# Mean pooling over 512 MiB: loads of 63 KB per partition in pairs of one run, double stores of 31.5 KB runs, the last double store on SP's queue

## The chip, the cores and the metric

The kernel runs on one core of one Trainium2 chip. A core has several engines that run side by side; three matter here. VectorE (DVE) does the additions, ScalarE (ACT) the scaling and also issues most stores, and SyncE (SP) issues the loads. The data are moved between the chip's main memory (HBM) and the core's working memory (SBUF, 128 partitions) by 16 DMA engines. Each transfer that SP or ACT issues is cut into one packet per contiguous run and shared among the 16 DMA engines; SP's transfers stand in one queue on each of them (q1 in the profile), ACT's in another (q10).

The metric is the device time of one execution in microseconds (us); lower is better. The kernel before has a median of 1554.53 us over three runs (1554.42 to 1555.98).

## The reference

The input x has 64 x 256 rows of 8192 float32 numbers, 536.87 MB. Kernel size and stride are both 4, so each output is the mean of four neighbours, no two outputs share an input, and the output has 64 x 256 x 2048 numbers, 134.22 MB.

```python
x = np.random.randn(64, 256, 8192).astype(np.float32)   # kernel_size = stride = 4
out_len = (length - kernel_size) // stride + 1           # 2048
for i in range(out_len):
    start = i * stride
    output[:, :, i] = np.mean(x[:, :, start : start + kernel_size], axis=2)
```

Since the row length is a multiple of 4, the whole input can be treated as one flat run of numbers, and every stretch whose length is a multiple of 4 becomes a stretch of a quarter of its length in the flat output.

## The kernel before

The flat input has 134,217,728 numbers, 1,048,576 for each of the 128 partitions. It is cut into 64 blocks of 128 x 16384 numbers (`FULL`), each one contiguous piece of memory of 8 MB, in which partition p takes the p-th 64 KB. The last two blocks are laid out together: partition p has one run of 128 KB there (`xe`, line 67), whose first half is block 62 and whose second half is loaded in three pieces of 8192, 4608 and 3584 numbers (`TAIL`).

`fetch(i)` (line 72) takes one of two input buffers (`xin`, `bufs=2`) and lets SP issue the load of block i. Two loads are issued ahead. The loop at line 84 then handles one block a turn:

- `sums` (line 55): two DVE additions. The first (line 57) adds even and odd neighbours in place, 16384 numbers to 8192; the second (line 58) adds neighbours again and writes 4096 sums into half of an output buffer `ot` (8192 numbers a partition, two buffers).
- `fetch(i + 2)`: SP issues the load of block i + 2 into the buffer that has just been summed. SP's instruction waits until DVE is done with that buffer.
- `nc.scalar.mul` (line 97): ACT multiplies by 1/4 in place, and `store` (line 50) lets ACT issue the store.

The first 8 blocks (`SINGLE`) are stored one by one. From then on two blocks are scaled and stored together once the second is summed: 8192 numbers a partition, but in memory they are two separate runs of 16 KB, since the two blocks lie apart (`"(b p m) -> p b m"`, line 52).

At the end, block 62 is scaled by ACT (line 92) and not stored yet. The three pieces of the last block follow (line 101): the first is summed, scaled by ACT and stored by SP together with block 62, as one run of 24 KB (line 110); the second is scaled by ACT and stored by ACT; the last is scaled by DVE (line 105), which has just summed it, and stored by ACT (line 112).

The order on each engine is the program's order. SP's queue holds all loads and the one store at line 110; ACT's queue holds the other 37 stores. A planner fills in the waits from the use of the buffers: a load waits for the sums that read its buffer before, and a sum into `ot` waits for the store that read that buffer before.

Of the kernel before, what the change touches and what calls it, by code (L numbers as in the profile page):

```python
# [1 line left out]

# [4 lines left out]


FULL = 16384
PAIR = 2  # L10

SINGLE = 8

TAIL = (8192, 4608, 3584)


@with_exitstack
def kernel(
    ctx: ExitStack,
    tc: tile.TileContext,  # L20
    x: bass.AP,
    kernel_size: bass.AP,
    stride: bass.AP,
    out: bass.AP,
):
    nc = tc.nc
    K, S = int(kernel_size), int(stride)
    assert K == S == 4
    B, C, L = x.shape
    assert L % K == 0  # L30
    P = nc.NUM_PARTITIONS
    dt = x.dtype
    add, mult = mybir.AluOpType.add, mybir.AluOpType.mult


    xf = x.rearrange("b c l -> (b c l)")
    of = out.rearrange("b c l -> (b c l)")
    blocks = B * C * L // P // FULL
    assert blocks * P * FULL == B * C * L and sum(TAIL) == FULL and blocks % PAIR == 0
    M = FULL // K  # L40

    pin = ctx.enter_context(tc.tile_pool(name="xin", bufs=2))
    pout = ctx.enter_context(tc.tile_pool(name="res", bufs=2))

    def load(xt, a, w):

        src = xf[P * a : P * (a + w)].rearrange("(p m) -> p m", p=P)
        nc.sync.dma_start(out=xt, in_=src)  # L48

    def store(engine, o, a, n, m):  # L50

        dst = of[P * a : P * (a + n * m)].rearrange("(b p m) -> p b m", b=n, p=P)
        engine.dma_start(out=dst, in_=o.rearrange("p (b m) -> p b m", b=n))

    def sums(xt, o):
        w = xt.shape[1]
        nc.vector.tensor_tensor(out=xt[:, : w // 2], in0=xt[:, ::2], in1=xt[:, 1::2], op=add)  # L57
        nc.vector.tensor_tensor(  # L58
            out=o, in0=xt[:, : w // 2 : 2], in1=xt[:, 1 : w // 2 : 2], op=add
        )  # L60

    xs = {}

    end = blocks - 2
    xe = xf[P * end * FULL :].rearrange("(p m) -> p m", p=P)
    oe = of[P * end * M :].rearrange("(p m) -> p m", p=P)
    edges = [FULL + sum(TAIL[:i]) for i in range(len(TAIL) + 1)]
    pieces = list(zip(edges[:-1], edges[1:]))  # L70

    def fetch(i):
        xt = xs[i] = pin.tile([P, FULL], dt, name="xt")
        if i < end:
            load(xt[:, :], i * FULL, FULL)
        elif i == end:
            nc.sync.dma_start(out=xt[:, :], in_=xe[:, :FULL])
        else:
            for a, b in pieces:
                nc.sync.dma_start(out=xt[:, a - FULL : b - FULL], in_=xe[:, a:b])  # L80

    fetch(0)
    fetch(1)
    for i in range(blocks - 1):
        k = i % PAIR
        if k == 0:
            ot = pout.tile([P, PAIR * M], dt, name="ot")
        sums(xs.pop(i)[:, :], ot[:, k * M : (k + 1) * M])
        if i + 2 < blocks:
            fetch(i + 2)  # L90
        if i == end:
            nc.scalar.mul(ot[:, :M], ot[:, :M], 1.0 / K)  # L92
        elif k == PAIR - 1 or i < SINGLE:

            n = 1 if i < SINGLE else PAIR
            o = ot[:, (k + 1 - n) * M : (k + 1) * M]
            nc.scalar.mul(o, o, 1.0 / K)  # L97
            store(nc.scalar, o, (i + 1 - n) * M, n, M)

    xt = xs.pop(blocks - 1)  # L100
    for a, b in pieces:
        o = ot[:, a // K : b // K]
        sums(xt[:, a - FULL : b - FULL], o)
        if b == 2 * FULL:
            nc.vector.tensor_scalar(out=o, in0=o, scalar1=1.0 / K, scalar2=None, op0=mult)  # L105
        else:
            nc.scalar.mul(o, o, 1.0 / K)  # L107
        if a == FULL:

            nc.sync.dma_start(out=oe[:, : b // K], in_=ot[:, : b // K])  # L110
        else:
            nc.scalar.dma_start(out=oe[:, a // K : b // K], in_=o)


# [1 line left out]
_INS = ['x', 'kernel_size', 'stride']  # L116
_OUTS = [((64, 256, 2048), 'float32')]

_NUMBERS = {'kernel_size': 4, 'stride': 4}


# [26 lines left out]
```

## Time and profile before

| what | value |
|---|---|
| median of three runs | 1554.53 us (1554.42 to 1555.98) |
| profiled execution, first to last instruction (span) | 1552.9 us |
| what lies around the span, against the median | 1.6 us (1554.53 - 1552.9) |
| DVE busy | 840.8 us, 54% |
| ACT busy | 226.7 us, 15% |
| bytes read and written | 536.87 MB and 134.22 MB, 432 GB/s over the span |
| DMA packets | 18435 |
| one full block on DVE, line 57 and line 58 | 8692 ns and 4425 ns |
| scaling of a double on ACT | 7029 ns |
| full load, issue to landing | 35.1 us (median of 63) |
| double store, issue to landing | 51.8 us (median of 27) |
| single store, issue to landing | 31.7 us (median of 8) |

The profile is of one execution. It lists no time of its own for that execution beside the span; the difference to the median of the runs is what is put around the span here.

How to read it: a row of the timeline has the start of an instruction, its duration, its engine and line, and in brackets how long the engine had been idle before it and what ended that. A row of the windows has a stretch of time, the busy time of DVE, ACT and POOL in it with the number of instructions, the granted TensorE clock (TensorE is not used here), the share of the 16 DMA engines that was busy, and the GB/s they moved. The share can come out slightly above 1.00, since a packet's record can overlap the next one's. The chain is the work that ended last, followed back from the end; it goes through whatever released the next step, which need not be the resource that limits the whole. The trace also holds a record of each DMA packet, with its size, its queue, its start and its duration.

### The profile page before, as it was taken

The numbers are of one execution on the slowest core, as the hardware profiler recorded it, in microseconds if no ns is written. First come the engines' busy times: TensorE is split into PE (matmuls) and PEld (weight loads), VectorE is DVE, ScalarE is ACT, GpSimd is POOL, SyncE is SP. The second block draws the span as 40 slices with busy tenths as digits, with TensorE's granted clock in tenths as the row PEclk, the third lists the DMA queues.
The fourth block names the chain that finished last, engine by engine and source line by source line (L and its number), as shares of the span: only waits on it lengthen the run. The fifth ranks groups of instructions, "written<-read, shape, count | busy, mean of one in ns | idle before, by whom it ended". The sixth has DMA issues, their size and how long they took to land.

```text
span 1552.9 us, 476 instructions
## 1 busy us (share of the span) xinstructions
DVE 840.8 (54%) x133; ACT 226.7 (15%) x39; POOL 0.2 (0%) x4
## 2 busy tenths in 40 slices
DVE  3646556546465464654646546455464554645546
ACT  1111101110111101111011110111101111011111
POOL 0000000000000000000000000000000000000000
DMA  9999999999999999999999999999999999999999
GB/s 415 421 433 439 439 439 439 412 446 436 421 433 433 445 437 438 433 422 430 439 437 434 437 427 425 439 432 438 438 419 435 434 436 438 442 425 435 425 432 406
DMA packets 18435, 671.12 MB, mean 432 GB/s; under 512 B 1664, under 2 KB 1664, under 8 KB 1920
## 3 DMA queue, kind: packets, MB, share of 16 engines
q1 hardware_dynamic: 9648, 540.02, 80.3%
q10 hardware_dynamic: 8784, 131.07, 19.7%
q14 instruction: 3, 0.02, 0.0%
HBM read 536.87 MB, written 134.22 MB: 432 GB/s over the span
## 4 chain that ended last, share of the span: by engine, by line
DMA 73%; DVE 26%; issue 0%; SPq 0%
DMA xt<-in_x_dram 73%; DVE xt L57 18%; DVE ot L58 9%; SPq L80 0%; DVE ot L105 0%; SPq L48 0%
## 5 line engine op out<-in xcount | busy, mean ns | idle before, releaser
L57 DVE TENSOR_TENSOR xt<-xt 128x8192 f32<-128x8192 f32 (+1 forms) x66 | 556.6, 8433 | 701.4 <-DMA xt<-in_x_dram 701.4
L97 ACT ACTIVATE ot<-ot 128x8192 f32<-128x8192 f32 (+1 forms) x35 | 218.7, 6249 | 1289.1 <-DVE ot L58 1289.1
L58 DVE TENSOR_TENSOR ot<-xt 128x4096 f32<-128x4096 f32 (+1 forms) x66 | 283.5, 4296 | 3.9
L92 ACT ACTIVATE ot<-ot 128x4096 f32<-128x4096 f32 x1 | 3.6, 3617 | 16.6 <-DVE ot L58 16.6
L107 ACT ACTIVATE ot<-ot 128x2048 f32<-128x2048 f32 (+1 forms) x2 | 3.1, 1537 | 10.2 <-DVE ot L58 10.2
L97 ACT ACT_TABLE_LOAD x1 | 1.3, 1283 | 0.7 <-PEq L129 0.7
L105 DVE TENSOR_SCALAR ot<-ot 128x896 f32<-128x896 f32 x1 | 0.6, 627 | 0.0
L129 POOL MEMSET const-bfloat16-1.0<- 128x1 bf16 x1 | 0.1, 102 | 0.0
L129 POOL MEMSET const-uint8-127<- 128x1 uint8 x1 | 0.1, 102 | 0.0
L129 POOL MEMSET const-float32-0.0<- 128x1 f32 x1 | 0.1, 99 | 0.2 <-issue 0.2
L129 POOL MEMSET const-float32-1.0<- 128x1 f32 x1 | 0.1, 99 | 0.0
## 6 DMA issues: line engine op xcount, KB each, us to landing
out_dram<-ot ACTq DMA_DIRECT2D x27, 4096.0 KB, 51.8
out_dram<-ot ACTq DMA_DIRECT2D x8, 2048.0 KB, 31.7
xt<-in_x_dram SPq DMA_DIRECT2D x1, 4096.0 KB, 24.9
out_dram<-ot SPq DMA_DIRECT2D x1, 3072.0 KB, 13.6
xt<-in_x_dram SPq DMA_DIRECT2D x1, 2304.0 KB, 35.0
xt<-in_x_dram SPq DMA_DIRECT2D x1, 1792.0 KB, 38.6
xt<-in_x_dram SPq DMA_DIRECT2D x63, 35.1
out_dram<-ot ACTq DMA_DIRECT2D x1, 576.0 KB, 7.6
```

The lines of the kernel that those rows point to most:

```text
L57: nc.vector.tensor_tensor(out=xt[:, : w // 2], in0=xt[:, ::2], in1=xt[:, 1::2], op=add)
L58: nc.vector.tensor_tensor(out=o, in0=xt[:, : w // 2 : 2], in1=xt[:, 1 : w // 2 : 2], op=add)
L92: nc.scalar.mul(ot[:, :M], ot[:, :M], 1.0 / K)
L97: nc.scalar.mul(o, o, 1.0 / K)
L105: nc.vector.tensor_scalar(out=o, in0=o, scalar1=1.0 / K, scalar2=None, op0=mult)
L107: nc.scalar.mul(o, o, 1.0 / K)
L129: nc = _bacc.Bacc("TRN2", target_bir_lowering=False, num_devices=1)
```

## The change

The block becomes 128 x 16128 numbers, 63 KB a partition. The work is now a list of stretches, each of them one contiguous piece of memory in which a partition has one run:

- `FIRST`: one block by itself, stored by itself (4032 numbers a partition).
- 31 `PAIR`s of two blocks: partition p has a run of 126 KB, of which the first load takes the first 63 KB and the second load the rest. The means of both are one run of 31.5 KB a partition and go out in one store.
- `LAST`: one block and the three pieces of 8192, 4608 and 3584 numbers, as one run a partition.

That makes 1 + 62 + 1 = 64 full loads and 3 pieces (64 x 16128 + 16384 = 1,048,576 numbers a partition). The buffers keep their sizes (16384 and 8192 numbers a partition, two of each). The steps of a turn keep their order: sums, the fetch two ahead, scaling, store. The order at the end is another: the last pair's double store is issued by SP, after the loads of the last block and of the three pieces (`i == len(fills) - 3`); the last block is stored by itself, by SP; each of the three pieces is stored by itself, by ACT. The last piece is scaled by DVE as before.

```diff
-FULL = 16384
-PAIR = 2
-SINGLE = 8
-TAIL = (8192, 4608, 3584)
+FULL = 16128
+FIRST = (FULL,)
+PAIR = (FULL, FULL)
+LAST = (FULL, 8192, 4608, 3584)
+PAIRS = 31
...
+    for widths in stretches:
+        n = sum(widths)
+        xs = xf[P * at : P * (at + n)].rearrange("(p m) -> p m", p=P)
+        os = of[P * at // K : P * (at + n) // K].rearrange("(p m) -> p m", p=P)
+        edges = [sum(widths[:i]) for i in range(len(widths) + 1)]
+        pieces = list(zip(edges[:-1], edges[1:]))
+        if widths is LAST:
+            fills += [(xs, os, pieces[:1], n), (xs, os, pieces[1:], n)]
+        else:
+            fills += [(xs, os, [p], n) for p in pieces]
+        at += n
...
+        xt = tiles[i] = pin.tile([P, 16384], dt, name="xt")
+        for a, b in pieces:
+            nc.sync.dma_start(out=xt[:, a - base : b - base], in_=xs[:, a:b])
+
+    def scale_and_store(engine, ot, os, a, b, last=False):
+        o = ot[:, a // K : b // K]
+        if last:
+            nc.vector.tensor_scalar(out=o, in0=o, scalar1=1.0 / K, scalar2=None, op0=mult)
         else:
...
+            nc.scalar.mul(o, o, 1.0 / K)
+        engine.dma_start(out=os[:, a // K : b // K], in_=o)
...
+    for i, (xs, os, pieces, n) in enumerate(fills):
+        base = pieces[0][0]
+        if base == 0:
+            ot = pout.tile([P, 8192], dt, name="ot")
+        xt = tiles.pop(i)
+        end = i >= len(fills) - 2
+        for a, b in pieces:
+            sums(xt[:, a - base : b - base], ot[:, a // K : b // K])
+            if end:
+                engine = nc.sync if a == 0 else nc.scalar
+                scale_and_store(engine, ot, os, a, b, last=b == n)
+        if i + 2 < len(fills):
+            fetch(i + 2)
+        if not end and pieces[-1][1] == n:
...
+            engine = nc.sync if i == len(fills) - 3 else nc.scalar
+            scale_and_store(engine, ot, os, 0, n)
```

More of the change, by code (lines that the diff above doesn't have):

```diff
@@ L37 @@
     of = out.rearrange("b c l -> (b c l)")
-    blocks = B * C * L // P // FULL
-    assert blocks * P * FULL == B * C * L and sum(TAIL) == FULL and blocks % PAIR == 0
-    M = FULL // K
+    stretches = [FIRST] + [PAIR] * PAIRS + [LAST]
+    assert sum(map(sum, stretches)) * P == B * C * L
     pin = ctx.enter_context(tc.tile_pool(name="xin", bufs=2))
     pout = ctx.enter_context(tc.tile_pool(name="res", bufs=2))
[L45 to L53, printed above, removed]
     def sums(xt, o):
@@ L60, in sums @@
         )
[L62 to L70, printed above, removed]
-    def fetch(i):
[L73 to L101, printed above, removed]
+    fills = []
+    at = 0
+    for widths in stretches:
[9 more added lines that the diff above has]
+        at += n
+    tiles = {}
+    def fetch(i):
+        xs, _, pieces, _ = fills[i]
+        base = pieces[0][0]
[3 more added lines that the diff above has]
+    def scale_and_store(engine, ot, os, a, b, last=False):
         o = ot[:, a // K : b // K]
-        sums(xt[:, a - FULL : b - FULL], o)
-        if b == 2 * FULL:
+        if last:
             nc.vector.tensor_scalar(out=o, in0=o, scalar1=1.0 / K, scalar2=None, op0=mult)
@@ L107 @@
             nc.scalar.mul(o, o, 1.0 / K)
[L108 to L112, printed above, removed]
+        engine.dma_start(out=os[:, a // K : b // K], in_=o)
+    fetch(0)
+    fetch(1)
+    for i, (xs, os, pieces, n) in enumerate(fills):
+        base = pieces[0][0]
+        if base == 0:
[12 more added lines that the diff above has]
+            scale_and_store(engine, ot, os, 0, n)
 _INS = ['x', 'kernel_size', 'stride']
```

## The prediction

> **What bounds the kernel now.** I read the page's head first (busy shares, DMA rate), then its chain, then the windows, then the chain and the timeline at three places: the start, one steady stretch, the end.
>
> ```profile
> DVE 840.8 (54%) x133; ACT 226.7 (15%) x39; POOL 0.2 (0%) x4
> DMA packets 18435, 671.12 MB, mean 432 GB/s; under 512 B 1664, under 2 KB 1664, under 8 KB 1920
> q1 hardware_dynamic: 9648, 540.02, 80.3%
> q10 hardware_dynamic: 8784, 131.07, 19.7%
> ```
>
> No compute engine is full, and the two data queues together hold the 16 DMA engines for 100.0% of the span. q1 is SP's queue (the loads), q10 ACT's (the stores). The chain says "DMA 73%; DVE 26%", which looks as if DVE shared the bound. It does not: the chain goes through DVE because SP issues load i+2 when DVE has summed tile i, while load i+1 is still moving. The windows show this.
>
> ```profile
> 300.00:400.00 100.00, 52.47 (x8) 14.06 (x2) 0.00 (x0) 1.00 1.01 435
> 700.00:800.00 100.00, 55.69 (x10) 14.06 (x2) 0.00 (x0) 1.00 1.00 433
> 1300.00:1400.00 100.00, 55.77 (x9) 14.06 (x2) 0.00 (x0) 1.00 1.00 434
> 1500.00:1520.00 20.00, 9.58 (x2) 7.03 (x1) 0.00 (x0) 1.00 1.00 433
> 1520.00:1540.00 20.00, 14.81 (x5) 5.53 (x2) 0.00 (x0) 1.00 1.00 429
> 1545.00:1552.90 7.90, 1.11 (x2) 0.00 (x0) 0.00 (x0) 1.00 0.69 291
> ```
>
> The last two columns are the DMA share and GB/s: 1.00 and about 433 everywhere, with a hole only in the last 7.9 us. So time can come from three places alone: fewer bytes (none here: both kernels read 536.87 MB and write 134.22 MB), less cost per packet, or less idle time at the ends.
>
> What a packet costs, apart from its bytes, comes from two cadences. The landing of a load is where DVE's next line-57 add starts.
>
> ```profile
> 22.62 8.69 DVE L57 TENSOR_TENSOR xt<-xt 128x8192 f32<-128x8192 f32 x1 [22.62 <-DMA xt<-in_x_dram]
> 41.93 8.69 DVE L57 TENSOR_TENSOR xt<-xt 128x8192 f32<-128x8192 f32 x1 [6.17 <-DMA xt<-in_x_dram]
> ...
> 1542.33 2.02 DVE L57 TENSOR_TENSOR xt<-xt 128x1792 f32<-128x1792 f32 x1 [0.17 <-DMA xt<-in_x_dram]
> ...
> 1545.51 0.63 DVE L105 TENSOR_SCALAR ot<-ot 128x896 f32<-128x896 f32 x1
> ```
>
> The timeline above gives start, duration, engine, line and, in brackets, the idle time; the chain below gives start, duration and work.
>
> ```profile
> 763.73 8.70 DVE xt L57
> ...
> 860.41 8.70 DVE xt L57
> ```
>
> Before the first store, one load takes 41.93 - 22.62 = 19.31 us: per DMA engine 8 packets of 65,536 B and one for the semaphore. In the steady stretch four loads and two stores take 860.41 - 763.73 = 96.68 us, 48.34 us a pair: per engine 16 load packets, 16 store packets of 16,384 B and 3 semaphore packets, 35 packets, 1,310,720 B. Two equations with a rate r and a cost c per packet: 19.31 = 524,288/r + 9c and 48.34 = 1,310,720/r + 35c give r = 27.22 B/ns and c = 5.2 ns. The trace's records of single packets agree: 65,536 B took 2418 ns, 16,384 B 611, 3,584 B 140, which is 27.2 B/ns and 8.6 ns besides; the records overlap a little, which is why the two shares can add up to more than 1.00. From the first data packet to the last in these records is 1550.0 us; a rate of 27.2 B/ns needs 1542.0 us for an engine's 41.94 MB. Take off 0.9 us of slow first packets (3.0 to 3.4 us each) and 1.2 us in which engines had finished one after another at the end, and 5.9 us are left for 1152 packets on each engine: 5.1 ns. I use that.
>
> The Trainium skill, DMA: Bandwidth & Descriptors, in "Where 436 GB/s comes from", makes the ceiling 16 ports of 32 B at 850 MHz, 435.2 GB/s; the steady rows (433 to 435) lie just under it, so the trace agrees.
>
> **The change part by part.** The sum goes against the profiled execution: span 1552.9 us. Its own time is not listed apart from the span; the median of the three runs, 1554.53, lies 1.6 us above it, and I carry that 1.6 over.
>
> *Packets.* Loads: 64 of 63 KB a partition and 3 tail pieces, 67 x 128 = 8576 data packets (66 x 128 = 8448 before). Stores: 1 single, 31 doubles now in one run, 4 at the end, 36 x 128 = 4608 (8192 before, each double being two 16 KB runs a partition). Semaphore packets: 103 DMAs x 16 = 1648 (104 x 16 = 1664). Sum 14,832 against 18,432 outside the small third queue, 927 against 1152 an engine. 225 packets fewer at 5.1 ns: **-1.1 us**. Bounds: 0 if the fixed cost hangs on bytes or on the count of loads, -1.9 us at the 8.6 ns that a single record shows. I take 5.1 because it is the mean over the whole execution.
>
> *Compute.* DVE adds as many elements in one pair of instructions more: 65,536-byte tiles cost 8.69 + 4.42 us, so 63 KB tiles 8.56 + 4.36. ACT's scaling of a double takes 7.03 x 63/64 = 6.92 us; 8 singles become doubles. None of it is on the path while a load is queued. The cover: load i+2 is issued 13.0 us after load i lands, and load i+1 needs 19.0 us (19.31 x 63/64) even with no store beside it. That leaves 6 us, less 1.4 us from an issue to its first packet (issue at 0.73, first packet near 2.1) and about 1 us of spread between engines. If the cover were gone, each microsecond missing would cost up to 1 us in each of 60 loads; I cost it at nothing.
>
> *Store order in the steady stretch.* In the records load and store packets alternate, so a 64 KB and a 16 KB packet give stores a fifth of the rate, and a double store needs 16 x (2.418 + 0.611) = 48.5 us, near the 51.8 us to landing that the page shows. With 63 KB and 31.5 KB packets it needs 8 x (2.380 + 1.194) = 28.6 us, about 31 to landing. The output buffer is wanted again some 62 us after the first scaling, so no new wait. The engines do the same bytes either way: 0.
>
> *The seam at the end.* The second of the last pair now stores through SP, behind the load of the last 63 KB block and the three pieces; on SP's queue the next store (of that block) waits behind it for ACT, and nothing else does. ACT's queue is left with the three small stores. The last loads no longer share the engines with a store, so the last one lands earlier. Remaining then: 4.13 + 2.06 + 1.05 + 0.59 + 0.46 = 8.29 MB, 19.1 us at 434 GB/s, where the kernel before had some 9 us left. So the last landing comes about 10 us earlier, near 1532, and DVE's end is covered: block (12.9 us) and first piece (6.7) make it late, pieces two and three follow, done about 8 us after the last landing, when SP's queue still has 10 us of stores. What is late next is the engines' own store work, so the 10 us buy nothing. Left to win is the idle end: of the 7.9 us at a share of 0.69, 2.4 us are idle, most of it after the last packet and in the spread of 1.2 us. The last packets stay the 3.5 KB ones of the same last store. Bounds: -0.7 (spread gone) to +0.5 (19 us at the 422 GB/s which 291/0.69 makes of that window, 2.6% under 433). I take **0**, between them.
>
> *Start.* Same first load but for 1 KB. Only one store instead of eight comes early; the engines have loads queued meanwhile. 0.
>
> Sum: 1552.9 - 1.1 = 1551.8 span, 1554.53 - 1.1 = **1553.4 us**.
>
> The Trainium skill, DMA: Bandwidth & Descriptors, "Why small descriptors are slow", puts the fixed cost at about 3 cycles a packet, 3.5 ns at its 850 MHz; by it the packets would save 0.8 us and the sum be 1553.7. The cadence says 5 ns, and the measurement goes first.
>
> **Rivals.**
>
> 1. *No saving.* The 31.5 KB runs are cut in two on the way, or the fixed cost is not a packet's. Against it: records of 14,336, 18,432, 24,576 and 32,768 B each are one packet. Then 8 more load packets an engine and the end's bound: 1554.5 to 1555.1. Chance 0.12.
>
> 2. *Slower: the new pitch.* Loads of a pair read 63 KB of every 126 KB instead of one closed block, so the engines walk other addresses. It decides when it costs 3.1 + 1.1 = 4.2 us, 8 ns on each of an engine's 512 full load packets (0.35%). For it: the window 1520 to 1540, in which the last block and pieces with a pitch of 128 KB land, has 429 GB/s. Against it: the 128 full packets of that block took 2418 ns each, as all others. Priced at 429 against 433 over the kernel: 671.1/0.429 - 671.1/0.433 = 14.5 us, 1553.4 + 14.5 = 1568. Chance 0.09. [...]
>
> 3. *Faster: the mixing was the cost.* If what the mixed stretch loses against loads alone is paid in the alternation of queues, it could shrink further: a pair costs 48.34 - 2.5 x 19.31 = 0.07 us more than loads alone, 32 pairs make 2.1 us. With the end's spread of 1.2 and half of the loads' own 2.2 us (0.035 us above 27.2 B/ns, x 64) it is 4.4 us: 1550.1. All of this would have to come together. Chance 0.05.
>
> **How the numbers follow.** Forecast (1551.9 to 1554.5): 0.74. It is taken from 1554.53 with the largest gains, -1.9 and -0.7, at its low end and no gain at its high one. Rival 1 adds 0.12 up to 1555.1. The range 1551.8 to 1555.9 holds these with the spread of the runs shown (1554.42 to 1555.98), and leaves rivals 2 and 3 out. 0.2% is 3.1 us, about what a measurement of this kernel can tell from no change: below 1551.4 faster, above 1557.6 slower. Forecast and rival 1 both lie within: 0.86, of which I give 0.01 to faster for the forecast's tail. Same 0.85, slower 0.09 (rival 2), faster 0.06 (rival 3 and that tail).
>
> **What would show it.** Packets near 14,835, 432 to 433 GB/s, DMA share 1.00 up to the last 2 or 3 us. Landing of a double store from 51.8 to about 31 us. DVE still idle for landings alone, and the last line-57 add starting near 1532 instead of 1542, with no earlier end in proportion. Two loads, one store and their pair taking 47.56 us (1,290,240 B at 27.2 B/ns and 27 packets at 5.1 ns): four loads and two stores in 95.1 us. The prediction is wrong if a stretch has a share of 1.00 at under 430 GB/s (longer packets, rival 2), if shares under 0.97 appear between loads (the cover of 6 us was too thin), or if more than 3 us go idle at the end.

## The result: slower by 0.7%

The changed kernel took 1565.55 us in the median of four runs (1561.93 to 1568.02), the kernel before 1554.52. The ratio is 1.0068, with a 95% interval of 1.0056 to 1.0080. A second measurement of the same code (e14 below) gave 1570.12, 1.0103 (1.0086 to 1.0120). The prediction was 1553.4 and no change that can be told; the time lies above its range of 1551.8 to 1555.9.

The page of the changed kernel has the packets that were forecast, and still no compute engine is full. Busy times, packets and the two data queues:

```profile
DVE 840.7 (54%) x135; ACT 226.1 (14%) x36; POOL 0.2 (0%) x4
DMA packets 14835, 671.12 MB, mean 430 GB/s; under 512 B 1648, under 2 KB 1648, under 8 KB 1904
q1 hardware_dynamic: 9936, 543.07, 80.8%
q10 hardware_dynamic: 4896, 128.03, 19.0%
out_dram<-ot ACTq DMA_DIRECT2D x30, 4032.0 KB, 32.4
```

14,835 packets as forecast, and a double store lands 32.4 us after its issue (forecast: about 31). But the mean rate is 430 GB/s and not 432. The windows show where (the last two columns are the DMA share and GB/s):

```profile
200.00:300.00 100.00, 51.67 (x8) 13.84 (x2) 0.00 (x0) 1.00 1.00 434
400.00:500.00 100.00, 56.20 (x9) 13.84 (x2) 0.00 (x0) 1.00 1.00 434
900.00:1000.00 100.00, 55.71 (x9) 13.84 (x2) 0.00 (x0) 1.00 1.00 428
1100.00:1200.00 100.00, 55.64 (x9) 13.84 (x2) 0.00 (x0) 1.00 1.00 430
1300.00:1400.00 100.00, 51.67 (x8) 13.84 (x2) 0.00 (x0) 1.00 0.99 427
1550.00:1562.30 12.30, 0.00 (x0) 0.00 (x0) 0.00 (x0) 1.00 0.58 244
```

Up to about 600 us the DMA engines move 434 GB/s, after that 427 to 434, at a share of 0.99 to 1.01 up to 1500 us: the engines are as busy as before and get less done. At the end 12.3 us have a share of 0.58 (before: 7.9 us at 0.69). The chain gives the same by the pair; each of these lines is DVE's first add (line 47) on the second block of a pair, first early, then late in the execution:

```profile
134.08 8.57 DVE xt L47
...
181.67 8.57 DVE xt L47
...
229.32 8.57 DVE xt L47
...
276.96 8.57 DVE xt L47
...
324.56 8.57 DVE xt L47
```
```profile
1234.89 8.57 DVE xt L47
...
1282.66 8.57 DVE xt L47
...
1330.69 8.57 DVE xt L47
...
1378.47 8.57 DVE xt L47
...
1426.55 8.57 DVE xt L47
```

Early a pair takes (324.56 - 134.08)/4 = 47.62 us, against 47.56 forecast. Late it takes (1426.55 - 1234.89)/4 = 47.92 us.

The trace's records of single packets say which packets are longer. In the kernel before a full load packet took 2418 ns nearly always; only 22 of 8000 after the start were more than 2% longer. In the changed kernel the usual 63 KB packet took 2380 ns, but 404 of 8128 were more than 2% longer, up to 3728 ns. Some 70 of these lie at the first two stores; the next ten starts of a store bring only a few, and the bulk comes after about 600 us. Nearly all belong to the second load of a pair and lie where the double store of the pair before begins: each engine's load packet that is under way just before its first store packet, and often the next. In the middle of a store nearly all packets have their usual length.

With these records the difference between the two profiled executions can be added up (the changed kernel's took 1564.11 us, so the table does not hold the rest up to its median). The columns are us from the first data packet to the last, per engine; "lengthened" is the time by which packets exceed the usual length of their size; "idle" is engine time without a packet, most of it in the last 10 us:

| term | before | changed |
|---|---|---|
| bytes at 27.2 B/ns | 1542.0 | 1542.0 |
| packets per engine x 5.1 ns | 1152: 5.9 | 927: 4.7 |
| slow first packets | 0.7 | 0.7 |
| lengthened packets | 0.6 | 8.1 |
| idle | 1.1 | 3.9 |
| sum; measured | 1550.3; 1550.0 | 1559.4; 1559.3 |

The packets saved 1.2 us, as forecast. Lengthened packets took back 7.5 and the uneven end 2.8. (The prediction took 0.9 us for the slow first packets; with the table's terms a packet costs 4.8 ns in the kernel before and 4.9 in the changed one, which is why the sums come out slightly high.)

### The profile page after: what moved, and what is told of

It is laid out like the page before. It is cut to its first block, busy times and chain, and to the rows that moved or that the text cites. A ratio compares the mean times of both kernels' runs of the same rounds, so it can differ in the third digit from the quotient of the medians.

```text
span 1562.3 us, 477 instructions
## 1 busy us (share of the span) xinstructions
DVE 840.7 (54%) x135; ACT 226.1 (14%) x36; POOL 0.2 (0%) x4
## 2 busy tenths in 40 slices
DMA packets 14835, 671.12 MB, mean 430 GB/s; under 512 B 1648, under 2 KB 1648, under 8 KB 1904
## 4 chain that ended last, share of the span: by engine, by line
DMA 71%; DVE 27%; issue 0%; DVEq 0%; SPq 0%
DMA xt<-in_x_dram 71%; DVE xt L47 18%; DVE ot L48 9%; DVEq L48 0%; DVE ot L80 0%; SPq L75 0%
## 5 line engine op out<-in xcount | busy, mean ns | idle before, releaser
L47 DVE TENSOR_TENSOR xt<-xt 128x8064 f32<-128x8064 f32 (+2 forms) x67 | 556.7, 8309 | 705.1 <-DMA xt<-in_x_dram 705.1
L82 ACT ACTIVATE ot<-ot 128x8064 f32<-128x8064 f32 (+3 forms) x35 | 224.8, 6422 | 1320.6 <-DVE ot L48 1320.6
L48 DVE TENSOR_TENSOR ot<-xt 128x4032 f32<-128x4032 f32 (+2 forms) x67 | 283.6, 4234 | 4.1
## 6 DMA issues: line engine op xcount, KB each, us to landing
out_dram<-ot ACTq DMA_DIRECT2D x30, 4032.0 KB, 32.4
```

Source lines behind the costliest of these rows:

```text
L48: nc.vector.tensor_tensor(out=o, in0=xt[:, : w // 2 : 2], in1=xt[:, 1 : w // 2 : 2], op=add)
```

## The experiments

The theories, as they stood at the start. **A**: a store that starts on an empty store queue lengthens the load packets under way. The kernel before does this once or twice, because its double store takes as long as a pair (51.8 us to landing, 48.3 a pair); the changed kernel does it in each pair, because its stores take 31.5 KB for 63 KB of load and are through after 30 us. **B**: the loads' pitch of 126 KB. **C**: packets off the 64 KB grid. **D**: the new order at the end. A "restart" below is such a start on an empty store queue. The times of the full runs differ by about 1% or less, so what is compared is, beside the time, the lengthened packets of one profiled execution each; between executions of one kernel these vary (8.1 us in the changed kernel above, 10.1 in e14).

### e1: the double store as two transfers of 15.75 KB packets

```diff
-        engine.dma_start(out=os[:, a // K : b // K], in_=o)
+        h = 2 if b - a == 2 * FULL else 1
+        w = (b - a) // K // h
+        for j in range(h):
+            engine.dma_start(
+                out=os[:, a // K + j * w : a // K + (j + 1) * w],
+                in_=o[:, j * w : (j + 1) * w],
+            )
```

> The changed kernel, but a double store goes out as two transfers of 15.75 KB a partition instead of one of 31.5 KB; loads and end unchanged. Theory A (onset): each time the store queue starts again after having run empty, the load packet under way on each engine is lengthened, which costs the changed kernel some 8 us over 31 pairs. Here a double store needs 16 x (2.380 + 0.601) = 47.7 us beside loads, and a pair takes 47.6, so the queue does not run empty: mean full load packet 2383 ns or less (2397 in the changed kernel), time 1553 to 1556. Theory B (the loads' pitch of 126 KB) and theory C (packets of 63 KB off the 64 KB grid): loads unchanged, so 2395 to 2400 ns and 1562 to 1568.

Measured: 1557.98 us, 1.0019 (1.0010 to 1.0028). That is 2 us above theory A's range and 4 us below that of B and C. The mean full load packet is 2383 ns, 1.0 us of lengthened packets in all after the start, and the pairs are even. In the records the time in each pair without a store packet falls from 23 us in the changed kernel to 2.4 us or less, one load packet. The same place in the chain as above:

```profile
1228.08 8.57 DVE xt L47
...
1275.69 8.57 DVE xt L47
...
1323.30 8.57 DVE xt L47
...
1370.91 8.57 DVE xt L47
...
1418.52 8.57 DVE xt L47
```

Each pair takes 47.61 us. The loads are those of the changed kernel, with pitch and 63 KB packets, so neither B nor C explains its loss. The kernel has 279 packets more on each engine than the changed one, 1206 against 927, and is 7.6 us faster. It stays 3.4 us over the kernel before; by the same sum its profiled execution has 0.3 us from packets, 0.4 from lengthened packets and 0.9 from idle time. That execution was the fastest of ten, and what the others have besides is not seen.

### e2: 64 KB blocks at a pitch of 128 KB

```diff
-FULL = 16128
+FULL = 16384
...
-    stretches = [FIRST] + [PAIR] * PAIRS + [LAST]
+    stretches = [PAIR] * PAIRS + [LAST]
```

> The changed kernel with blocks of 64 KB and no single block in front: 31 pairs of 64 KB loads at a pitch of 128 KB, double stores in one run of 32 KB, end unchanged. Theory A: a double store needs 8 x (2.418 + 1.213) = 29 us of a 48.2 us pair, so the store queue runs empty in each pair and the loss stays: 1561 to 1568, full load packets 10 to 20 ns over 2418 in the mean. Theory B: a pitch again, 1560 to 1570. Theory C: back on the 64 KB grid, 1553 to 1556.

Measured: 1569.63 us, 1.0091 (1.0068 to 1.0115); the mean full load packet is 2449 ns instead of 2418, and 15.7 us of packets are lengthened on an engine. Both are more than theory A had said (up to 1568 us and 20 ns longer packets), and by this time alone B would do as well. The size off the grid (C) is not the cause: on the grid the loss is at least as large.

```profile
300.00:400.00 100.00, 52.48 (x8) 16.29 (x3) 0.00 (x0) 1.00 1.00 431
400.00:500.00 100.00, 52.47 (x8) 15.90 (x3) 0.00 (x0) 1.00 1.00 429
1200.00:1300.00 100.00, 52.47 (x8) 14.06 (x2) 0.00 (x0) 1.00 0.99 425
```

Here the loss is there from the first pairs on: 429 to 431 GB/s already between 300 and 500 us.

### e3: 63 KB blocks, each one closed piece of memory

```diff
+            if n == 2 * FULL:
+                xs = xf[P * at : P * (at + n)].rearrange("(b p m) -> p b m", b=2, p=P)
+                os = of[P * at // K : P * (at + n) // K].rearrange("(b p m) -> p b m", b=2, p=P)
             fills += [(xs, os, [p], n) for p in pieces]
...
```

(The lines left out take the load and the store from these pieces.)

> Blocks of 63 KB as in the changed kernel, but each block one closed piece of memory as in the kernel before, so a double store is one transfer of two runs of 15.75 KB a partition; end unchanged. Theory A: the store queue does not run empty (47.7 us against 47.6), 1553 to 1556, load packets 2383 ns or less. Theory B: no pitch, 1553 to 1556. Theory C: still 63 KB packets, 1562 to 1568.

Measured: 1556.81 us, 1.0011 (1.0002 to 1.0021), mean full load packet 2383 ns, 0.9 us of lengthened packets; a double store lands late again:

```profile
out_dram<-ot ACTq DMA_DIRECT2D x30, 4032.0 KB, 51.3
```

B is undone here, C is not, and the loss is gone; with e1 this leaves the stores.

### e4: the last double store on ACT's queue

```diff
-            engine = nc.sync if i == len(fills) - 3 else nc.scalar
-            scale_and_store(engine, ot, os, 0, n)
+            scale_and_store(nc.scalar, ot, os, 0, n)
```

> The changed kernel with the last double store on ACT's queue, beside the last loads, instead of on SP's queue behind them. The changed kernel has 3.7 us of idle engine time at its end against 1.2 before. Theory D (the seam makes the end uneven): 2 to 3 us less than the changed kernel, 1559 to 1565. Theory A without D: the end's idle time comes from engines that the onsets have driven apart, so the time stays at 1562 to 1568 and one engine still lags 4 us or more.

Measured: 1569.91 us, 1.0099 (1.0083 to 1.0114), beside 1570.12 for the changed kernel measured again. The end has 3.1 us of idle time in its last 10 us, hardly less than the changed kernel's 3.7. D falls. The time lies above both forecasts, and 15.8 us of packets are lengthened. Until its end this is the changed kernel, yet its engines drift apart, and longer packets and a lower rate appear, much earlier:

```profile
200.00:300.00 100.00, 51.67 (x8) 13.84 (x2) 0.00 (x0) 1.00 0.99 426
```

So when the loss sets in differs between executions of the same steps.

### e5, e6, e7: short loads beside short stores

If A is right as it stands, a restart costs whatever the packets' size. In e5, the kernel before loads 64 KB in two transfers of 32 KB, so its 16 KB stores take a third of the engines and run dry. e6 adds `SINGLE = 62`, so the same stores come in more starts. e7 takes e5 and cuts the stores to 8 KB packets, so the queue stays busy.

```diff
-        nc.sync.dma_start(out=xt, in_=src)
+        for h in range(0, w, w // 2):
+            nc.sync.dma_start(out=xt[:, h : h + w // 2], in_=src[:, h : h + w // 2])
...
-            nc.sync.dma_start(out=xt[:, :], in_=xe[:, :FULL])
+            for h in (0, FULL // 2):
+                nc.sync.dma_start(out=xt[:, h : h + FULL // 2], in_=xe[:, h : h + FULL // 2])
```

> The kernel before with each full load issued as two transfers, the first and the second 32 KB of each partition's 64 KB; stores as before, 16 KB a packet. 63 x 9 packets more on each engine at 5.1 ns make 2.9 us, 1557.4 without any other loss. Theory A (each restart of an empty store queue costs about 8/31 = 0.26 us): a double store now needs 16 x (1.213 + 0.611) = 29 us of 48.4, so the queue runs empty 35 times (8 singles, 27 doubles), 9 us more: 1563 to 1571. Theory A' (it is the long store packet of 31.5 KB and not the empty queue): 1556 to 1559.

> As e5, but the first 62 blocks are all stored one by one, so the same 16 KB packets go out in 62 separate starts instead of 35. Theory A: 62 restarts at 0.26 us, 16 us over 1557.6: 1568 to 1580, clearly slower than e5. Theory E (not the restart but the time during which stores take a third of the engines costs, whatever the number of starts): the same as e5 within 2 us.

> As e5, but each store goes out as two transfers with packets of 8 KB, so a double store needs 32 x (1.213 + 0.309) = 48.7 us beside the loads and the queue does not run empty. About 550 store packets more on each engine, 2.8 us. Theory A: only the packets' cost, 1557.4 + 2.8 = 1560 (1558 to 1562.5), faster than e5 with more packets. Theories A' and E: slower than e5 by those 2 to 3 us.

Measured: e5 1559.51 us (1.0033), e6 1560.50 (1.0039), e7 1560.55 (1.0039). The queue does run dry in e5; its double store lands after 31.8 us:

```profile
out_dram<-ot ACTq DMA_DIRECT2D x27, 4096.0 KB, 31.8
out_dram<-ot ACTq DMA_DIRECT2D x8, 2048.0 KB, 18.3
```

Yet all packets together are lengthened by only 2.3 us on an engine in e5 and 1.8 in e6, and 1.1 and 0.7 of it fall in the first 45 us; each later start costs 0.04 us or less. Theory A as I had put it falls, with its 9 and 16 us. (e6 is within 1 us of e5, as theory E said, but neither has a loss of the changed kernel's size.) e7 has 0.5 us of lengthened packets and 1098 packets more on each engine than the kernel before: at 5.1 ns that is 5.6 us, measured 1560.55 - 1554.45 = 6.1. The packet's price holds far outside the range it was read from. That e7 would be faster than e5, as theory A said, did not come true.

### e8: the new end on the kernel before

```diff
+            nc.sync.dma_start(out=oe[:, :M], in_=ot[:, :M])
...
-            store(nc.scalar, o, (i + 1 - n) * M, n, M)
+            store(nc.sync if i == end - 1 else nc.scalar, o, (i + 1 - n) * M, n, M)
...
-        if a == FULL:
-
-            nc.sync.dma_start(out=oe[:, : b // K], in_=ot[:, : b // K])
-        else:
-            nc.scalar.dma_start(out=oe[:, a // K : b // K], in_=o)
+        nc.scalar.dma_start(out=oe[:, a // K : b // K], in_=o)
```

> The kernel before with the changed kernel's end alone: the last double store on SP's queue behind the last loads, block 62 stored by itself by SP, the first piece by ACT. Theory D (the seam costs): 1556 to 1558, as the two variants of 63 KB without restarts (1556.8 and 1558.0) still lie 2 to 3 us over the kernel before. Without D: 1553.5 to 1555.

Measured: 1554.55 us, 1.0001 (0.9992 to 1.0010). The third part of the change neither costs nor gains, as forecast, and the 3.4 and 2.3 us that e1 and e3 keep are not from it.

### e9, e10, e11: which of three conditions is needed

All start from e2, which has long loads (64 KB), long stores (32 KB) and a restart in each pair. e9 makes the stores short by leaving out the second half of each pair's means, e10 makes the loads short, and e11 keeps both long and removes the restart: it reads half of the input and stores each result twice. e9 and e11 do other work in all, so their times are not compared, and each is a single execution.

```diff
 e9
+        if b - a == 2 * FULL:
+            b, o = a + FULL, o[:, : FULL // K]
 e10
-            nc.sync.dma_start(out=xt[:, a - base : b - base], in_=xs[:, a:b])
+            c = FULL // 2 if b - a == FULL else b - a
+            for h in range(a, b, c):
+                nc.sync.dma_start(out=xt[:, h - base : h - base + c], in_=xs[:, h : h + c])
 e11
-PAIRS = 31
+PAIRS = 15
...
-        engine.dma_start(out=os[:, a // K : b // K], in_=o)
+        for d in os:
+            engine.dma_start(out=d[:, a // K : b // K], in_=o)
```

> As e2 (64 KB loads in pairs, 31 pairs), but of each double store only the first half is stored, so 16 KB packets instead of 32 KB; the second half's means are left out, 65 MB less, and the time itself (about 1404 without loss) is not to be compared. The store queue still starts from empty in each pair (8 x (2.418 + 0.611) = 24 us of a 43 us pair). Theory P (a restart costs much only where store packets are long): lengthened load packets add under 3 us on an engine in all. Theory L (it costs much where load packets are long, 64 KB): 8 to 15 us as in e2, mean full load packet 2433 to 2448 ns.

> As e2, but each full load goes out as two transfers of 32 KB a partition; double stores stay one run of 32 KB. 567 load packets more on each engine at 5.1 ns, 2.9 us. A double store needs 8 x (1.213 + 1.213) = 19 us of 48, so 31 restarts with long store packets and short load packets. Theory P: the restarts cost what they cost in e2 (15 us on an engine there), so 1565 to 1575. Theory L: the restarts cost under 3 us, so 1556 to 1559.5.

> As e2, but only the first half of the input is read, and each store goes out twice, to the two halves of the output, so the second half of the output is a copy and not its means. A double store now needs 16 x (2.418 + 1.213) = 58.1 us beside a pair of 58.1, so long store packets alternate with long load packets and the queue does not run empty. About 932 us without loss. Theories P and L with the restart as the cause: after the first start full load packets stay at 2418 ns, mean under 2423. Theory F (long store packets lengthen the loads wherever they run, restart or not): mean full load packet 2433 ns or more, as in e2 (2448).

The lengthened packets in us per engine, beside the number of restarts:

| run | load, store packets | restarts | lengthened |
|---|---|---|---|
| e2 | 64 KB, 32 KB | 31 | 15.7 |
| e9 | 64 KB, 16 KB | 31 | 1.2 |
| e10 | 32 KB, 32 KB | 31 | 3.2 |
| e5 | 32 KB, 16 KB | 35 | 2.3 |
| e11 | 64 KB, 32 KB | queue stays busy | 1.0 |

In e9 and e11 most of it lies at the first start (60 of the 63 and 16 of the 20 load packets that are more than 2% longer). In e10 30 of 34 such packets lie there, but they make only 0.9 of its 3.2 us; the rest is spread over the later restarts, some 0.07 us each where e2 loses 0.5. So e9's stores and e11's busy queue remove the loss, and e10's loads remove most of it. Both P and L, in which one long packet was enough, fall, and F with them. e10 took 1560.08 us (1.0035), 9.6 less than e2 with 567 packets more on each engine. In e11 a store follows another in the queue and lands late; the rate stays up:

```profile
out_dram<-ot ACTq DMA_DIRECT2D x28, 4096.0 KB, 54.0
```
```profile
300.00:400.00 100.00, 44.60 (x8) 14.06 (x2) 0.00 (x0) 1.00 1.01 438
400.00:500.00 100.00, 44.31 (x7) 7.03 (x1) 0.00 (x0) 1.00 1.00 433
500.00:600.00 100.00, 47.52 (x8) 14.06 (x2) 0.00 (x0) 1.00 1.00 435
700.00:800.00 100.00, 51.32 (x8) 7.89 (x2) 0.00 (x0) 1.00 1.00 435
```

### e12: every second double store cut

```diff
-        h = 2 if b - a == 2 * FULL else 1
+        h = 2 if cut else 1
...
+            scale_and_store(engine, ot, os, 0, n, cut=i > 0 and i // 2 % 2 == 0)
```

(Shown against e1; at the end of the function every second pair is now stored with `cut` set.)

> The changed kernel, but every second pair's double store (15 of 31) goes out as two transfers of 15.75 KB packets. A cut store needs 47.7 us of a 47.6 us pair, so the uncut store after it finds the queue still busy; the queue starts from empty only where a cut store begins. So half of the stores keep long packets, yet no restart has a long packet. Theory R (it takes a restart, long load packets and long store packets together): no loss but that of e1: 1556 to 1558.5, mean full load packet 2384 ns or less. Theory F (long store packets bring the loss wherever they run): half of it, about (1565.5 + 1558)/2 = 1561.8, 2388 to 2395 ns.

Measured: 1560.19 us (1557.34 to 1562.49), 1.0034 (1.0022 to 1.0046), between the two forecasts. The mean full load packet, 2386 ns, lies between them too; 2.3 us are lengthened, 1.2 more than in e1, and 4.1 us idle, 2.1 more. The queue did what was meant from the second pair on: in the records no store packet runs for 19 to 24 us before a cut store, but for only 1.6 to 4.0 us before an uncut one, much as between the two halves of a cut store. (The first pair's uncut store alone starts from empty.) The longer packets of the second half lie mostly in the first 14 us after a cut store has started on an empty queue, about half of them 10 to 14 us in, and hardly any where a long store follows. So long store packets without a restart do not lengthen packets here either. But a restart with short ones, next to long stores, is not free, as R had said it would be.

### e13: stores of 24 KB packets

```diff
+        if b - a == 2 * FULL:
+            b = a + FULL + FULL // 2
+            o = o[:, : (b - a) // K]
```

> As e2, but of each double store only the first three quarters are stored, 24 KB packets; the last quarter's means are left out, 32 MB less, so the time is not to be compared. 31 restarts as in e2 and e9. If the cost of a restart grows with the store packet: between e9 (1.2 us of lengthened load packets on an engine at 16 KB) and e2 (15 us at 32 KB), 4 to 11 us. If it sets in at once: under 2.5 us or over 12 us.

(Against e2; the last quarter of each pair's means is left out, and this too is a single execution.) Measured: 1.1 us of lengthened packets, as in e9. A store still lands far within a pair (30.0 us, a pair some 46), so the restarts are there. Up to 24 KB the loss does not grow with the store packet; it sets in somewhere between 24 KB and 31.5 KB.

### e14: the changed kernel again

> The changed kernel once more, unaltered, beside e12 on the same chip. Its four runs lay between 1561.9 and 1568.0, those of the kernel that differs only in its end (e4) between 1567.9 and 1572.5. Theory R: 1560 to 1573 again, with lengthened load packets in the pairs' second loads from a different pair on than in the first profile.

Measured: 1570.12 us (1566.14 to 1572.33). Up to 500 us its rate is 434 GB/s, then 427 to 433, as in the first profile; that the loss would begin at another pair did not come true between these two:

```profile
200.00:300.00 100.00, 51.67 (x8) 13.85 (x2) 0.00 (x0) 1.00 1.00 434
400.00:500.00 100.00, 55.77 (x9) 13.85 (x2) 0.00 (x0) 1.00 1.00 434
700.00:800.00 100.00, 53.55 (x9) 16.07 (x3) 0.00 (x0) 1.00 1.00 427
1000.00:1100.00 100.00, 55.49 (x9) 13.85 (x2) 0.00 (x0) 1.00 1.00 429
```

The records of the semaphore packets, one per engine at the end of each transfer, show how it starts. After the first store one engine ends its loads about 2 us behind the other 15, most of which stay within 0.6 us of each other. In e9 and e13 that lag stays where it is, under 2.8 us to the end of the loads. In these two profiles of the changed kernel it grows from restart to restart, from 3.2 to 3.6 us in the third to fifth pair to 4.1 and 4.7 us near 490 us, and reaches 7 us near 600; from then on the other engines have longer packets and drift apart too. In e2 and e4 there is no such laggard (the 16 end their loads within 0.6 us of each other through the third pair); all drift from the fourth pair on, to the same 7 us. In e12, with half of the restarts, the lag grows more slowly and reaches 6.9 us near 1250 us, after which most of its later longer packets come; in e1 it stays at 2.8. At 7 us it stops, near the 6 us of cover that the prediction worked out: an engine further ahead would have no load queued. That the stop is due to this was not tried. Nor do the runs say why engines fall further back at a restart with 31.5 KB store packets and not with 24 KB, or whether the spread lengthens the packets or the longer packets make the spread: that stays open.

## Why the prediction was wrong, step by step

- *Packets, -1.1 us*: right. 927 against 1152 on each engine; by the terms of the table above a packet costs 4.8 to 5.0 ns in every full run from 909 (e2) to 2250 (e7) packets, so 5.1 was close. (Of the stores before, 8192 is a slip for 8320; the total of 18,432 is right.)
- *Compute, nothing*: right. DVE still waits for landings alone, and 6.92 us of scaling lie beside transfers.
- *Store order in the steady stretch, "The engines do the same bytes either way: 0"*: this is the step that failed. The alternation, the store's 28.6 us and its landing were right. The conclusion was not: a store that is through after 28.6 us of a 47.56 us pair leaves the store queue empty for the rest, and I gave that no price and no bounds. The kernel before had shown a price in the records: 19 load packets of up to 3018 ns at its first store, 0.6 us of lengthened packets in all, though its next start from empty, at 262 us, cost nothing. Thirty more like the first would have made a bound of 18 us. The measured term is +7.5 us in lengthened packets.
- *The seam, 0*: right as far as it is the order of the queues (e8, e4). The end as a whole was off by 2.8 us of idle time, and this follows how far apart the engines arrive there: the last load ends on them over 1.1 us in the kernel before, 1.2 in e3, 2.3 in e1 and 4.7 in the changed kernel, and the idle time is 1.1, 1.2, 2.0 and 3.9. So it is in the main a consequence of the step above. (More than 3 us idle at the end was named as a sign of being wrong, and it came.) The last load lands at 1542.2 and not near 1532; in e1, without the delays, at 1534.4. The last line-57 add (now line 47), by which the prediction wanted to see it, starts later still, at 1546.1 and 1537.2: it does not wait for the landing but for DVE's own sums before it, which the prediction had seen as late.
- *Rival 2, the pitch*: its sign came true (share 1.00 below 430 GB/s, packets longer by 16 ns in the mean where 8 decided), and 1568 was near. Its mechanism did not: e1 keeps the pitch without the loss, at 47.61 us a pair, so the near number was luck. The Trainium skill, DMA: Bandwidth & Descriptors, "Latency and other measured facts", lists 207 GB/s at a row pitch of 512 KiB beside 214 where it calls the rate full, and no smaller pitch; no run here has a pitch of 512 KiB.

## What to carry to other kernels

Where transfers bound a kernel, look not only at bytes and packets but at whether a queue that shares the engines runs dry: here two short runs beside a long load kept it busy for almost exactly a period, and joining them saved 1.2 us and cost 10 in the profiled execution. A packet's time beside a load follows from its size (alternating packets), so the time in which the store queue is empty can be worked out ahead. Give every change of that pattern a bound from the nearest start in the trace, even where the bytes are the same.

## What the runs showed of the hardware

- A packet costs about 5 ns (4.8 to 5.0) besides its bytes at 27.2 B/ns, from 909 to 2250 packets on an engine; a single record shows 8.6 ns, and the records overlap a little.
- The loss needs three things together in the runs here: load packets of 63 or 64 KB, store packets of 31.5 or 32 KB, and a store queue that starts from empty. With any one of the three taken away (e9 and e13, e10, e11) packets are lengthened by 1.0 to 3.2 us on an engine, most of it at the first start except in e10, against 8.1 to 15.8 us with all three. e12, where restarts with short packets alternate with long stores, lies close to the former with 2.3 us.
- The engines do not stay in step: in the changed kernel, e1, e9, e12 and e13 one lags about 2 us after the first store. Where the loss is large (the changed kernel, e2, e4) the ends of a load drift apart to about 7 us, with or without such a laggard at first; where it is small they stay within 5 us, except in e12.
